# Output weights split beside two pairs of heads, and two output tiles split beside the last softmax sums, in a two-layer hybrid backbone

## The chip, the cores and the metric

One core of a Trainium2 chip runs the whole kernel in one launch. The metric is the device time of that launch in microseconds (us), the median of several runs. The engines are named as in the profile: PE is TensorE (PEld its weight loads, which overlap the matmuls), DVE is VectorE, ACT is ScalarE, POOL is GpSimd, and SP is the engine that only issues DMA transfers, in the order in which they stand in its queue.

## The reference, cut to what matters

The model has two layers. The change lies in the second half of the second one, attention over 1280 keys (256 of context, 1024 latent) for 1024 latent queries and 16 heads of 64 value columns:

```python
o = attend(q, k, v)                      # softmax(q k^T * SCALE) v, 16 heads
y = (o * silu(g)) @ w_out_mla            # 1024 x 1024
return layer_norm(ALPHA * h + gate * y, ln_g[1], ln_b[1])
```

Here `h` is the output of layer 0, itself a layer norm: `h = n * ln_g[0] + ln_b[0]`, with `n` kept in DRAM (`n_dr`).

## The kernel before, in words

All products that need float32 accuracy are made of three matmuls: an operand is split into a high part, rounded to the matmul's format (a cast, mostly on ACT), and a low part, the difference (a subtraction). The helper `split` (L80 to L82) does both, and `load` (L60) puts a DMA on SP's queue.

**Attention** runs over 8 pairs of heads (`p`), two halves of 512 queries (`hf`), and 10 key tiles (`kt`), so a pair has 20 steps (`g`). In a step `attend` (L1031) issues ten score matmuls into `s` (L1051), the exponential on ACT (`p`, L1053), and the running sum of the exponentials over the key tiles, which is the softmax's denominator: on POOL in pairs 0 to 6 (`ra`, L1057). In pair 7 the even key tiles are summed on POOL into `ra` and the odd ones on DVE into `rv` (L1061). Six buffers hold the exponentials. `pv` (L1064) multiplies them with the values into `po`. `finish` (L1070) gives the steps that end a half, done in the first steps of the next half: `rest` (the last two `pv`, and the gate `sgt` times `po` on DVE), `rows` (matmuls `rp` with ones that add the sums over the partitions, and a copy to `ri` on ACT), four `piece` (reciprocals on DVE), and `last` (`sgt` times `ri` on DVE, and the store to `o_dr` in DRAM).

Lists `near` and `far` hang other work on the steps. In pairs 0 to 6 this is the next pair's projections and its pass for the row maxima (`mx`, `m`). Pair 7 has no next pair; the **output weights** `wo1` are prepared there, in 8 slices of 128 rows: `wo1_load` (L1147) loads one, `wo1_high` (L1151) casts it on ACT, `wo1_low` (L1154) subtracts on POOL, or on DVE for three of the eight. They lie in the pool `fin1`, which takes the place of the projections' buffers.

**The output** has 8 tiles of 128 queries. `o_load` (L1103) reads a tile of all heads back from `o_dr` (`orw`), casts it (`oh`, ACT) and subtracts (`ol`, DVE). `out1` (L1185) is 48 matmuls into `yf` (L1191), 24 pairs of one for each half of the columns. Tile 0's load stands at the end of pair 7, and its matmuls are mixed with the steps that end the last half. All other buffers of this stage (the tiles' `oh` and `ol`, the residual `hres`, the vectors `g1bc`, `ln0`, `ln1`) are in the pool `fin`, which takes the place of attention's buffers. For each tile POOL makes the residual `hres` (L1216, L1217), and DVE makes `g1 * yf` (L1235), adds the residual (L1236), and norms (L1237 to L1246).

The order of PE, DVE, ACT and POOL in this part is the order in which the code issues (a manual schedule); SP's queue is ordered by the compiler's scheduler.

Of the kernel before, what the change touches and what calls it, by code (L numbers as in the profile page):

```python
# [54 lines left out]
def _body(ctx, tc, ap, out, dbg=None):  # L55
    nc = tc.nc
    V, S, G, TE = nc.vector, nc.scalar, nc.gpsimd, nc.tensor
    dbg = dbg or {}

    def load(o, i):  # L60
        nc.sync.dma_start(out=o, in_=i)

    def f(x):
        return x.bitcast(F32)

    def pool(name, bufs=1, space=None, side=None):
# [89 lines left out]
    gate_dr = dram.tile([2, 2, D], F32, name="gate_dr")  # L156
# [265 lines left out]
    for n in ("cos_h", "cos_l", "sin_h", "sin_l"):  # L422
        t = ft_p.tile([P, 2, 2, 256], F32R, name=n)
# [249 lines left out]
    qnh = [lat_p.tile([P, NL], F32R, name=f"qnh{k}") for k in range(2)]
    qnl = [lat_p.tile([P, NL], F32R, name=f"qnl{k}") for k in range(2)]
    kvh = lat_p.tile([P, T], F32R, name="kvh")
    kvl = lat_p.tile([P, T], F32R, name="kvl")
# [354 lines left out]
    def attend(p, hf, kt, st):  # L1031

        q, i = divmod(p, 2)
        c = slice(512 * hf, 512 * hf + 512)
        ks = slice(P * kt, P * kt + P)
        if kt == 0:
            st["sg"] = at.tile([P, 512], F32, tag="sgt", bufs=2, name=f"sgt{p}{hf}")
            load(st["sg"], sg_dr[p][:, c])
            st["o"] = o_ps.tile([P, 512], F32, tag="o", name=f"po{p}{hf}")
            st["ra"] = at.tile([P, 2, 512], F32, tag="ra", bufs=2, name=f"ra{p}{hf}")  # L1040
            if p == 7:
                st["rv"] = at.tile([P, 2, 512], F32, tag="rv", name=f"rv{hf}")
            st["e"] = []
        b = p % 2
        ps = s_ps.tile([P, 2, 512], F32, tag="s", name=f"s{p}{hf}{kt}")

        parts = ((Kh[b], Qh[b], 64), (Kh[b], Ql[b], 64), (Kl[b], Qh[b], 64), (KR1, R1[b], 64), (KR2, R2[b], 33))
        for j, (k, w, n) in enumerate(parts):
            for a in range(2):
                r = slice(64 * a, 64 * a + n)  # L1050
                TE.matmul(ps[:, a, :], k[r, ks], w[r, c], start=(j == 0), stop=(j == len(parts) - 1))  # L1051
        es = at.tile([P, 2, 512], F32, tag="p", bufs=PB, name=f"p{p}{hf}{kt}")
        S.activation(out=es, in_=ps, func=AF.Exp, scale=SCALE)  # L1053
        if kt:
            ra = st["ra"]
            if p < 7:
                G.tensor_tensor(out=ra, in0=st["e"][0] if kt == 1 else ra, in1=es, op=ALU.add)  # L1057
            elif kt > 1:

                ra = st["rv"] if kt % 2 else ra  # L1060
                (V if kt % 2 else G).tensor_tensor(out=ra, in0=st["e"][kt - 2] if kt < 4 else ra, in1=es, op=ALU.add)  # L1061
        st["e"].append(es)

    def pv(p, st, k):  # L1064
# [38 lines left out]
    def o_load(t, p):  # L1103
        orw = f1_p.tile([P, 8, P], F32, tag="raw", bufs=3, name=f"orw{t}")
        load(orw, o_dr.rearrange("k p t -> p k t")[:, :, P * t : P * t + P])
        oh = p.tile([P, 8, P], F32R, tag="oh", bufs=1 if t == 0 else 2, name=f"oh{t}")
        ol = p.tile([P, 8, P], F32R, tag="ol", bufs=1 if t == 0 else 2, name=f"ol{t}")
        split(oh, ol, orw, S, V)
        return oh, ol

    vt[1] = at.tile([P, NT, 256], F32, name="v_odd")
    tail = {}
    for p in range(8):

        near = [[] for _ in range(2 * NT)]
        far = [[] for _ in range(2 * NT)]
        if p < 7:
            prep = prep_pair(p + 1)
            mx = max_pass(p + 1)
            near[0] += prep[:2]  # L1120
            far[0] += prep[2:3]
            near[1] += prep[3:4]
            far[1] += prep[4:5]
            near[2] += prep[5:]
            at_ = [(g, b) for g in range(2, 2 * NT) for b in range(2) if not (g == 2 and b == 0) and (b == 0 or g % 2)]
            at_.insert(0, (2, 1))
# [12 lines left out]
        else:
            pr_c()  # L1140
            f1_p, f1_c = pool("fin1", 2, side="left")
            w1o = [f1_p.tile([P, D], F32R, bufs=1, name=f"w1oh{k}") for k in range(8)]
            w1p = [f1_p.tile([P, D], F32R, bufs=1, name=f"w1ol{k}") for k in range(8)]

            raws = {}

            def wo1_load(k):  # L1147
                raws[k] = f1_p.tile([P, D], F32, tag="raw", bufs=3, name=f"w1oraw{k}")
                load(raws[k], ap["wo1"][:, k, :])

            def wo1_high(k):  # L1151
                S.copy(out=w1o[k], in_=raws[k])

            def wo1_low(k):  # L1154
                (V if k % 3 == 1 else G).tensor_tensor(out=w1p[k], in0=raws[k], in1=f(w1o[k]), op=ALU.subtract)
                if k + 3 < 8:
                    wo1_load(k + 3)

            for k in range(3):
                wo1_load(k)  # L1160
            for k in range(8):
                far[2 * k + 2].append(lambda k=k: wo1_high(k))
                far[2 * k + 3].append(lambda k=k: wo1_low(k))
        for hf in range(2):
            st = {}
            for kt in range(NT):
                g = NT * hf + kt
                attend(p, hf, kt, st)
                for u in near[g]:
                    u()  # L1170
                if kt > 2 and kt % 2:
                    pv(p, st, kt - 3)
                    pv(p, st, kt - 2)
                for u in tail.get(kt, ()):
                    u()
                for u in far[g]:
                    u()
                if p == 7 and g == 18:
                    o0 = o_load(0, f1_p)
            tail = finish(p, hf, st)  # L1180

    s_psc()
# [2 lines left out]
    def out1(oh, ol, ps, pieces, group, work={}):  # L1185
        for k in range(8):
            for u in work.get(k, ()):
                u()
            for a, b in ((oh, w1o), (oh, w1p), (ol, w1o)):
                for i in group:  # L1190
                    TE.matmul(ps[i], a[:, k, :], b[k][:, pieces[i]],  # L1191
                              start=(k == 0 and a is oh and b is w1o), stop=(k == 7 and a is ol))

    H2 = [slice(0, 512), slice(512, D)]
    y0 = f_ps.tile([P, D], F32, tag="y", name="yf0")
    out1(*o0, [y0[:, c] for c in H2], H2, range(2), {1: tail[1], 3: tail[3]})
# [6 lines left out]

    fp, fc = pool("fin", 2, side="right")
    ln1 = fp.tile([P, 2, D], F32, bufs=1, name="ln1")
    ln0 = fp.tile([P, 2, D], F32, bufs=1, name="ln0")
    g1 = fp.tile([P, D], F32, bufs=1, name="g1bc")
    load(g1, gate_dr[1][0:1, :].to_broadcast([P, D]))
    for t in range(8):
        if t:  # L1210
            oh, ol = o_load(t, fp)
        x = fp.tile([P, D], F32, tag="hres", name=f"hres{t}")
        load(x, n_dr[t])
        if t == 0:
            load(ln0, ap["lnw0"].to_broadcast([P, 2, D]))
        G.tensor_tensor(out=x, in0=x, in1=ln0[:, 0, :], op=ALU.mult)  # L1216
        G.tensor_tensor(out=x, in0=x, in1=ln0[:, 1, :], op=ALU.add)  # L1217
        if t == 0:
            load(ln1, ap["lnw1"].to_broadcast([P, 2, D]))
# [23 lines left out]
        for hf in range(2):  # L1243
# [128 lines left out]
```

## Time and profile before

| | us |
|---|---|
| median of 3 runs | 1477.8 (1475.59 to 1479.57) |
| the profiled execution: its own time | 1479.07 |
| its span, first to last instruction | 1477.3 |
| PE busy (whole span) | 1409.1 (95%) |
| DVE busy | 931.4 (63%) |
| POOL busy | 660.9 (45%) |
| ACT busy | 539.9 (37%) |

The span ends with these stretches, counted from its start: pair 6 of attention from about 1240, pair 7 from about 1307 to 1352, the output tiles from 1357, the end at 1477.3. Shares over the whole span say little about the last 125 us, where other engines set the time than in the stretches before, so the rows below are taken from that part. A row of the timeline gives start, duration, engine, line, operation and names, and in brackets how long the engine was idle before it and what released it.

### The profile page before, as it was taken

What the parts mean: (1) busy time and instruction counts of PE and PEld (TensorE: products, weight loads), DVE (VectorE), ACT (ScalarE), POOL (GpSimd) and SP (SyncE); (2) the same over time, 40 slices, a digit from 0 to 9 for tenths busy, and PEclk for the clock granted to TensorE, in tenths of its full rate; (3) what the DMA queues carried; (4) which work ended last, traced back from release to release, by engine and by line L of the source; (5) the groups of instructions that cost most, each with busy time, mean ns of one, the idle gap of its engine ahead of it and who ended that gap; (6) DMA issues with size and microseconds to landing.
All of it is one profiled execution on the core that took longest, in us unless ns stands there. A gap on an engine that the chain in (4) does not pass through costs nothing.

```text
span 1477.3 us, 19801 instructions
## 1 busy us (share of the span) xinstructions
PE 1409.1 (95%) x7912; PEld 1009.3 (68%) x7912; DVE 931.4 (63%) x1461; ACT 539.9 (37%) x664; POOL 660.9 (45%) x307
## 2 busy tenths in 40 slices
PE   6998999999999999998999999999999999998895
PEld 3776777787888788887976755655555555554674
DVE  5668878665765352239635365667566665767698
ACT  2276566666112221105421333443433434353110
POOL 1134334343211143303241187568767856675442
PEclk9999999999999999999999999999999999999998
DMA  8613233332303564210242211012101101033431
GB/s 307 232 51 110 97 111 111 111 103 76 123 29 126 188 192 140 92 52 22 89 137 71 72 33 51 15 37 59 39 22 38 57 16 37 15 95 113 159 131 74
DMA packets 65868, 134.09 MB, mean 91 GB/s; under 512 B 5864, under 2 KB 31720, under 8 KB 63472
## 3 DMA queue, kind: packets, MB, share of 16 engines
q1 hardware_dynamic: 63328, 124.83, 26.1%
q0 software_dynamic: 2016, 7.60, 1.4%
q8 instruction: 62, 1.02, 0.3%
q10 hardware_dynamic: 432, 0.39, 0.1%
q14 instruction: 30, 0.25, 0.1%
HBM read 101.14 MB, written 24.66 MB: 85 GB/s over the span
## 4 chain that ended last, share of the span: by engine, by line
PE 68%; DVE 20%; DMA 4%; issue 4%; ACT 2%; POOL 2%; SPq 0%; DVEq 0%; POOLq 0%; ACTq 0%
PE s L1051 11%; PE z L267 11%; PE y L646 10%; PE po L1067 9%; PE mx L976 6%; PE in1g L85 2%; PE in1g L87 2%; PE in1g L86 2%; DVE xc L317 2%; DVE hf L1246 1%; DVE th L362 1%; DVE gate L367 1%; DVE gate L378 1%; DVE hf L1236 1%; DMA woraw<-in_wo 1%
## 5 line engine op out<-in xcount | busy, mean ns | idle before, releaser
L1057 POOL TENSOR_TENSOR ra<-ra,p 128x1024 f32<-128x1024 f32 x112 | 269.2, 2403 | 96.3 <-ACT p L1053 93.1
L978 DVE TENSOR_REDUCE m<-mx 128x1 f32<-128x512 f32 (+1 forms) x384 | 210.1, 589 | 100.9 <-PE mx L976 100.5
L1053 ACT ACTIVATE p<-s 128x1024 f32<-128x1024 f32 x160 | 163.3, 1025 | 208.4 <-PE s L1051 208.3
L267 PE MATMUL z<-uh,w0h 128*128 128x512 f32 (+1 forms) x576 | 150.1, 368 | 4.3 <-ACT uh L76 4.3
L267 PE MATMUL z<-ul,w0h 128*128 128x512 f32 (+1 forms) x576 | 147.9, 362 | 0.0
L267 PE MATMUL z<-uh,w0l 128*128 128x512 f32 (+1 forms) x576 | 147.5, 361 | 0.0
L82 POOL TENSOR_TENSOR w0l<-w,w0h 128x1024 fp32r<-128x1024 f32 x24 | 63.9, 2664 | 185.4 <-DVE w0h L78 135.5
L267 PEld LDWEIGHTS z<-uh,w0h 128*128 128x128 f32 x576 | 98.7, 191 | 33.4 <-issue 10.7
L267 PEld LDWEIGHTS z<-ul,w0h 128*128 128x128 f32 x576 | 96.8, 190 | 18.6 <-issue 1.0
L267 PEld LDWEIGHTS z<-uh,w0l 128*128 128x128 f32 x576 | 96.4, 190 | 18.3 <-issue 2.0
L1051 PE MATMUL s<-R,KR 33*128 33x512 f32 (+1 forms) x640 | 101.5, 392 | 0.0
L345 ACT ACTIVATE gate<-gps,vec 128x512 f32<-128x512 f32 (+1 forms) x96 | 57.5, 616 | 104.3 <-PE gps L87 104.2
L976 PE MATMUL mx<-Kh,Qh 64*128 64x512 f32 (+1 forms) x384 | 83.4, 404 | 4.5 <-DVE m L978 4.5
L976 PEld LDWEIGHTS mx<-Kh,Qh 64*128 64x128 f32 x384 | 39.1, 185 | 69.4 <-DVE m L978 35.5
L1067 PE MATMUL po<-p,v_odd 128*64 128x512 f32 x320 | 77.5, 605 | 0.0
L1067 PE MATMUL po<-p,v_even 128*64 128x512 f32 x320 | 77.5, 605 | 0.0
L381 POOL TENSOR_TENSOR gate<-gate,gate 128x1280 f32<-128x1280 f32 x8 | 23.9, 2988 | 112.2 <-DVE gate L378 97.1
L976 PE MATMUL mx<-KR,R 64*128 64x512 f32 (+1 forms) x384 | 72.7, 356 | 0.0
L1051 PEld LDWEIGHTS s<-R,KR 33*128 33x128 f32 (+1 forms) x640 | 61.3, 184 | 13.1
L1051 PE MATMUL s<-Qh,Kh 64*128 64x512 f32 x320 | 69.9, 430 | 0.0
L649 DVE TENSOR_TENSOR n<-gbc,y 128x1024 f32<-128x1024 f32 x10 | 12.2, 1222 | 86.1 <-PE y L646 86.1
L1051 PE MATMUL s<-Ql,Kh 64*128 64x512 f32 x320 | 63.7, 391 | 0.0
(360 smaller groups left out, 3078.0 us busy)
## 6 DMA issues: line engine op xcount, KB each, us to landing
w<-in_w SPq DMA_DIRECT2D x24, 512.0 KB
adaw<-in_ada SPq DMA_DIRECT2D x32, 256.0 KB
adawm<-in_ada SPq DMA_DIRECT2D x8, 1024.0 KB
adawg<-in_ada_g SPq DMA_DIRECT2D x8, 1024.0 KB
y_dr<-sg SPq DMA_DIRECT2D x10, 640.0 KB
woraw<-in_wo SPq DMA_DIRECT2D x12, 512.0 KB
xt<-in_x_cm SPq DMA_DIRECT2D x8, 640.0 KB
yra<-y_dr SPq DMA_DIRECT2D x10, 512.0 KB
```

Of the source, the lines that this page charges most:

```text
L82: el.tensor_tensor(out=lo, in0=src, in1=f(hi), op=ALU.subtract)
L85: TE.matmul(o, lh, rh, start=start, stop=False)
L86: TE.matmul(o, lh, rl, start=False, stop=False)
L267: TE.matmul(z[:, a : a + n], wi[:, kt, :], ui[kt][:, a : a + n], start=(kt == 0 and ui is uh and wi is wh), stop=(kt == KT - 1 and wi is wl))
L345: S.activation(out=gt[d, g][:, a : a + n], in_=ps[:, :n], func=AF.Sigmoid, bias=vv("gateb", 4 * j + i))
L646: TE.matmul(ps[:, 512 * hf : 512 * hf + 512], a[k], b[k][:, 512 * hf : 512 * hf + 512], start=(k == 0 and a is yh and b is woh), stop=(k = ...
L976: TE.matmul(ps[a][:, :n], q[r, P * t : P * t + P], k[r, a0 : a0 + n], start=st, stop=not st)
L978: V.tensor_reduce(out=m3s[t][:, a, i : i + 1], in_=ps[a][:, :n], axis=AX.X, op=ALU.max)
L1051: TE.matmul(ps[:, a, :], k[r, ks], w[r, c], start=(j == 0), stop=(j == len(parts) - 1))
L1053: S.activation(out=es, in_=ps, func=AF.Exp, scale=SCALE)
L1057: G.tensor_tensor(out=ra, in0=st["e"][0] if kt == 1 else ra, in1=es, op=ALU.add)
L1067: TE.matmul(st["o"][64 * a : 64 * a + 64, :], quad[q][6][:, k, 128 * i + 64 * a : 128 * i + 64 * a + 64], st["e"][k][:, a, :], start=(k == ...
```

## The change

The high and low parts of slices 0 to 2 of the output weights are put into the buffers of the normed latents (`qnh`, `qnl`, `kvh`, `kvl`), which pair 7's projections read last, at the start of pair 6. Slice 3 and the raw slices have a new pool `we`, beneath attention's buffers. So slices 0 to 3 are cast and subtracted in pair 6 (steps 5, 9, 13, 17 and the one after each), slices 4 to 7 in pair 7, and all eight subtractions are on POOL. In pair 7 the sums move: POOL adds key tiles 0, 1, 2, 4, 5, 6, 8 and DVE the tiles 3, 7, 9. The buffers of `oh`, `ol`, `hres`, `ln0` and `g1bc` move to `fin1`. Tile 1 is loaded and split inside tile 0's matmuls, and the residuals of tiles 0 and 1 are issued there. There are two raw buffers where there were three.

```diff
+    we_p, we_c = pool("we", side="right")
+    def wo1_high(k):
+        if k < 2:
+            hi, lo = (lat_p.tile([P, D], F32R, tag=f"qn{x}{k}", name=f"w1o{x}{k}") for x in "hl")
+        elif k == 2:
+            hi, lo = (lat_p.tile([P, T], F32R, tag=f"kv{x}", name=f"w1o{x}{k}")[:, :D] for x in "hl")
+        else:
+            hi, lo = ((we_p if k == 3 else f1_p).tile([P, D], F32R, bufs=1, name=f"w1o{x}{k}") for x in "hl")
+        w1o[k], w1p[k] = hi, lo
+        S.copy(out=hi, in_=raws[k])
+    def wo1_low(k):
+        G.tensor_tensor(out=w1p[k], in0=raws[k], in1=f(w1o[k]), op=ALU.subtract)
+        if k + 2 < 8:
+            wo1_load(k + 2)
...
-            if p < 7:
+            if p < 7 or kt == 1:
                 G.tensor_tensor(out=ra, in0=st["e"][0] if kt == 1 else ra, in1=es, op=ALU.add)
-            elif kt > 1:
-                ra = st["rv"] if kt % 2 else ra
-                (V if kt % 2 else G).tensor_tensor(out=ra, in0=st["e"][kt - 2] if kt < 4 else ra, in1=es, op=ALU.add)
+            elif kt > 1 and kt != 3:
+                e, r = (V, st["rv"]) if kt in (7, 9) else (G, ra)
+                e.tensor_tensor(out=r, in0=st["e"][3] if kt == 7 else r, in1=es, op=ALU.add)
...
+    def residual(t):
+        x = f1_p.tile([P, D], F32, tag="hres", name=f"hres{t}")
+        load(x, n_dr[t])
+        G.tensor_tensor(out=x, in0=x, in1=ln0[:, 0, :], op=ALU.mult)
+        G.tensor_tensor(out=x, in0=x, in1=ln0[:, 1, :], op=ALU.add)
+        return x
...
+            g1 = f1_p.tile([P, D], F32, bufs=1, name="g1bc")
+            load(g1, gate_dr[1][0:1, :].to_broadcast([P, D]))
+            ln0 = f1_p.tile([P, 2, D], F32, bufs=1, name="ln0")
+            load(ln0, ap["lnw0"].to_broadcast([P, 2, D]))
+        if p > 5:
+            for k in range(4 * (p - 6), 4 * (p - 6) + 4):
+                g = 5 + 4 * k if p == 6 else 3 * k - 10
+                far[g].append(lambda k=k: wo1_high(k))
+                far[g + 1].append(lambda k=k: wo1_low(k))
+            if p == 6:
+                near[3] += [lambda k=k: wo1_load(k) for k in range(2)]
...
-    out1(*o0, [y0[:, c] for c in H2], H2, range(2), {1: tail[1], 3: tail[3]})
+    def second():
+        os_[1] = o_load(1)
+    out1(*os_[0], [y0[:, c] for c in H2], H2, range(2), {1: tail[1] + [second], 3: tail[3]})
+    xs = {t: residual(t) for t in range(2)}
```

PE's rows are the same, in the same order. Three places show what moves on the others. The first is DVE in pair 7, from the end of pair 6 to the first output tile's low part; names ending in 11209 (before) and 11222 (changed) are the gate of pair 7's first half. Before:

```order
L1061 TENSOR_TENSOR rv_11213<-rv_11213,p_11390 128x1024
L1077 TENSOR_TENSOR sgt_11209<-sgt_11209,po_11211 128x512
L1155 TENSOR_TENSOR w1ol_11199<-w1oraw_11322,w1oh_11191 128x1024
L1061 TENSOR_TENSOR rv_11404<-p_11430,p_11473 128x1024
L1092 RECIPROCAL ri_11459<-ri_11459 128x128 x3
L1061 TENSOR_TENSOR rv_11404<-rv_11404,p_11510 128x1024
L1092 RECIPROCAL ri_11459<-ri_11459 128x128
L1096 TENSOR_TENSOR sgt_11209<-ri_11459,sgt_11209 128x512
```

In the changed kernel, from the same `rv` on:

```order
L1083 TENSOR_TENSOR rv_11226<-rv_11226,p_11405 128x1024
L1099 TENSOR_TENSOR sgt_11222<-sgt_11222,po_11224 128x512
L1114 RECIPROCAL ri_11472<-ri_11472 128x128 x4
L1118 TENSOR_TENSOR sgt_11222<-ri_11472,sgt_11222 128x512
L1083 TENSOR_TENSOR rv_11417<-p_11486,p_11555 128x1024
L82 TENSOR_TENSOR ol_11579<-orw_11576,oh_11578 128x1024
```

A weight's subtraction and two sums that stood between the gate's two products are gone from there. The second place is POOL in pair 7, up to the first sum of its second half. Before (five of the rows; the first half's sum is `ra_11212`):

```order
L1061 TENSOR_TENSOR ra_11212<-p_11225,p_11256 128x1024
L1155 TENSOR_TENSOR w1ol_11195<-w1oraw_11203,w1oh_11187 128x1024
L1061 TENSOR_TENSOR ra_11212<-ra_11212,p_11297 128x1024
L1061 TENSOR_TENSOR ra_11212<-ra_11212,p_11335 128x1024
L1155 TENSOR_TENSOR w1ol_11197<-w1oraw_11207,w1oh_11189 128x1024
L1061 TENSOR_TENSOR ra_11212<-ra_11212,p_11373 128x1024
L1155 TENSOR_TENSOR w1ol_11198<-w1oraw_11284,w1oh_11190 128x1024
```

Changed, with the last subtraction of pair 6 ahead of it:

```order
L1043 TENSOR_TENSOR w1ol_11169<-w1oraw_10941,w1oh_11168 128x1024
L1079 TENSOR_TENSOR ra_10917<-ra_10917,p_11207 128x1024
L1079 TENSOR_TENSOR ra_11225<-p_11238,p_11251 128x1024
L1083 TENSOR_TENSOR ra_11225<-ra_11225,p_11270 128x1024
L1043 TENSOR_TENSOR w1ol_11274<-w1oraw_11070,w1oh_11273 128x1024
L1083 TENSOR_TENSOR ra_11225<-ra_11225,p_11312 128x1024
L1083 TENSOR_TENSOR ra_11225<-ra_11225,p_11327 128x1024
L1083 TENSOR_TENSOR ra_11225<-ra_11225,p_11349 128x1024
L1043 TENSOR_TENSOR w1ol_11336<-w1oraw_11194,w1oh_11335 128x1024
L1083 TENSOR_TENSOR ra_11225<-ra_11225,p_11386 128x1024
```

The half's sum now needs six adds with two subtractions among them, where it needed four and two. The third place is SP's queue where attention begins, around the store of the last gate (`sg_71`). Before:

```order
L61 DMA sg_dr<-sg_70_6591 128x512
L61 DMA sgt_6682<-sg_dr 128x512
L61 DMA R_6666<-roth_5789 32x1024 x2
L61 DMA sg_dr<-sg_71_6652 128x512
L61 DMA R_6667<-rotl_5790 32x1024
```

Changed:

```order
L61 DMA sg_dr<-sg_70_6591 128x512
L61 DMA w1oraw_10703<-in_wo 128x1024
L61 DMA w1oraw_10705<-in_wo 128x1024
L61 DMA sg_dr<-sg_71_6652 128x512
L61 DMA sgt_6685<-sg_dr 128x512
L61 DMA R_6669<-roth_5789 32x1024 x2
L61 DMA R_6670<-rotl_5790 32x1024
```

The first two weight slices are loaded there, and the rotary queries of pair 1 (`R`) now stand behind the store.

## Rows read from the trace of the kernel before

**Rows 1.** Windows: start:end, us, busy us (count) PE, PEld, DVE, ACT, POOL, clock, DMA share, GB/s

```profile
1240.00:1307.00 67.00, 66.42 (x438) 38.06 (x434) 41.01 (x74) 25.98 (x29) 47.51 (x20) 1.00 0.13 38
1307.00:1352.00 45.00, 44.95 (x276) 21.93 (x272) 36.36 (x22) 26.53 (x29) 35.41 (x14) 1.00 0.34 110
1352.00:1357.20 5.20, 0.00 (x0) 0.00 (x0) 2.37 (x1) 1.06 (x2) 1.29 (x1) 0.96 0.80 218
1357.20:1362.00 4.80, 4.76 (x14) 2.35 (x14) 2.36 (x2) 0.91 (x1) 0.00 (x0) 0.68 0.74 198
1432.00:1444.00 12.00, 11.85 (x51) 9.28 (x50) 11.96 (x14) 1.24 (x2) 5.51 (x3) 1.00 0.25 88
```

**Rows 2.** The chain that ended last, 1348 to 1392: start us, us, what

```profile
1348.06 1.91 DVE sgt L1096
...
1349.98 2.00 DMA o_dr<-sgt
...
1352.06 4.06 DMA orw<-o_dr
...
1356.14 1.05 ACT oh L76
...
1357.24 2.93 PE yf L1191 x6
...
1367.56 3.40 DVE ri L1092 x4
...
1374.03 7.62 DMA ln<-in_lnw
...
1386.72 5.68 DVE hf L1236 x2
```

**Rows 3.** Timeline of PE, from pair 7's first denominator to the fourth output tile's start

```profile
1333.33 1.08 PE L1084 MATMUL rp<-ra,ones 128*64 128x512 f32 x4
...
1350.01 1.94 PE L1067 MATMUL po<-p,v_odd 128*64 128x512 f32 x8
1357.24 1.22 PE L1191 MATMUL yf<-w1oh,oh 128*128 128x512 f32 x2 [5.29 <-ACT oh L76]
...
1373.81 0.63 PE L1191 MATMUL yf<-w1oh,oh 128*128 128x512 f32 x2
...
1396.21 0.63 PE L1191 MATMUL yf<-w1oh,oh 128*128 128x512 f32 x2
```

**Rows 4.** Timeline of DVE: a sum of pair 7, and steps of output tiles

```profile
1343.80 3.36 DVE L1061 TENSOR_TENSOR rv<-rv,p 128x1024 f32<-128x1024 f32 x1
...
1423.41 1.27 DVE L1235 TENSOR_TENSOR hf<-g1bc,yf 128x512 f32<-128x512 f32 x2
...
1453.70 5.71 DVE L1246 SCALAR_TENSOR_TENSOR hf<-hf,rsb,ln 128x512 f32<-128x512 f32 x2
...
1459.33 1.27 DVE L1235 TENSOR_TENSOR hf<-g1bc,yf 128x512 f32<-128x512 f32 x2
...
1464.67 1.41 DVE L1246 SCALAR_TENSOR_TENSOR hf<-hf,rsb,ln 128x512 f32<-128x512 f32 x2
```

**Rows 5.** Timeline of POOL, from pair 6's last sums to pair 7's last

```profile
1302.53 4.83 POOL L1057 TENSOR_TENSOR ra<-ra,p 128x1024 f32<-128x1024 f32 x2 [0.71 <-ACT p L1053]
...
1346.03 3.38 POOL L1061 TENSOR_TENSOR ra<-ra,p 128x1024 f32<-128x1024 f32 x1
1350.45 2.85 POOL L1061 TENSOR_TENSOR ra<-ra,p 128x1024 f32<-128x1024 f32 x1 [1.04 <-ACT p L1053]
```

**Rows 6.** Timeline of ACT in pair 7

```profile
1335.53 0.59 ACT L1087 COPY ri<-rp 128x512 f32<-128x512 f32 x1 [1.00 <-PE rp L1084]
...
1349.28 1.03 ACT L1053 ACTIVATE p<-s 128x1024 f32<-128x1024 f32 x1 [1.81 <-PE s L1051]
```

**Rows 7.** Timeline of SP's queue where attention begins

```profile
845.79 0.59 SPq L61 DMA_DIRECT2D R<-rotl  x1
```

**Rows 8.** Timeline of PE there: the first product with R

```profile
851.32 0.40 PE L976 MATMUL mx<-KR,R 64*128 64x512 f32 x2
```

More of the change, by code (lines that the diff above doesn't have):

```diff
@@ L672, in _body @@
     lat_p, lat_c = pool("lat", side="right")
[L673 to L676, printed above, removed]
+    qnh = [lat_p.tile([P, NL], F32R, tag=f"qnh{k}", name=f"qnh{k}") for k in range(2)]
+    qnl = [lat_p.tile([P, NL], F32R, tag=f"qnl{k}", name=f"qnl{k}") for k in range(2)]
+    kvh = lat_p.tile([P, T], F32R, tag="kvh", name="kvh")
+    kvl = lat_p.tile([P, T], F32R, tag="kvl", name="kvl")
     u1_p, u1_c = pool("u1", side="right")
@@ L1023, in _body, with wo1_load @@
     u1_c()
+    we_p, we_c = pool("we", side="right")
+    w1o, w1p, raws = {}, {}, {}
+    def wo1_load(k):
+        raws[k] = we_p.tile([P, D], F32, tag="raw", bufs=2, name=f"w1oraw{k}")
+        load(raws[k], ap["wo1"][:, k, :])
+    def wo1_high(k):
[11 more added lines that the diff above has]
+            wo1_load(k + 2)
     at, at_c = pool("at", side="right")
@@ L1101, in finish, with o_load @@
         return {1: [rest], 3: [rows], 4: [piece(0)], 5: [piece(1)], 6: [piece(2)], 7: [piece(3)], 8: [last]}
-    def o_load(t, p):
-        orw = f1_p.tile([P, 8, P], F32, tag="raw", bufs=3, name=f"orw{t}")
+    def o_load(t):
+        orw = we_p.tile([P, 8, P], F32, tag="raw", bufs=2, name=f"orw{t}")
         load(orw, o_dr.rearrange("k p t -> p k t")[:, :, P * t : P * t + P])
-        oh = p.tile([P, 8, P], F32R, tag="oh", bufs=1 if t == 0 else 2, name=f"oh{t}")
-        ol = p.tile([P, 8, P], F32R, tag="ol", bufs=1 if t == 0 else 2, name=f"ol{t}")
+        oh = f1_p.tile([P, 8, P], F32R, tag="oh", name=f"oh{t}")
+        ol = f1_p.tile([P, 8, P], F32R, tag="ol", name=f"ol{t}")
         split(oh, ol, orw, S, V)
         return oh, ol
+    def residual(t):
[4 more added lines that the diff above has]
+        return x
     vt[1] = at.tile([P, NT, 256], F32, name="v_odd")
@@ L1141, in _body @@
             f1_p, f1_c = pool("fin1", 2, side="left")
[L1142 to L1163, printed above, removed]
+            g1 = f1_p.tile([P, D], F32, bufs=1, name="g1bc")
[9 more added lines that the diff above has]
+                near[3] += [lambda k=k: wo1_load(k) for k in range(2)]
         for hf in range(2):
@@ L1178, in _body @@
                 if p == 7 and g == 18:
-                    o0 = o_load(0, f1_p)
+                    os_ = {0: o_load(0)}
             tail = finish(p, hf, st)
@@ L1205, in _body @@
     ln1 = fp.tile([P, 2, D], F32, bufs=1, name="ln1")
-    ln0 = fp.tile([P, 2, D], F32, bufs=1, name="ln0")
-    g1 = fp.tile([P, D], F32, bufs=1, name="g1bc")
-    load(g1, gate_dr[1][0:1, :].to_broadcast([P, D]))
+    load(ln1, ap["lnw1"].to_broadcast([P, 2, D]))
     for t in range(8):
[L1210 to L1219, printed above, removed]
+        oh, ol = os_.pop(t) if t in os_ else o_load(t)
+        x = xs.pop(t) if t in xs else residual(t)
         h = fp.tile([P, D], F32, tag="h", name=f"hf{t}")
@@ L1248, in _body @@
     fc()
+    we_c()
     f1_c()
```

## The prediction

> **What bounds the kernel now.** I read the windows first, for who is busy in each stretch. In pairs 6 and 7 TensorE works without a gap (66.42 of 67 us, 44.95 of 45), so nothing that shortens another engine's work there shortens the pair. From 1352.0 to 1357.2 TensorE does nothing; in the 4.8 us behind that gap its granted clock is 0.68, a mix of the levels 1.2 and 2.4 GHz, against 1.00 before. In an output tile of the steady end VectorE is busy 11.96 of 12 us and TensorE 11.85 [rows 1].
>
> The chain of waits says what the gap is made of. The gate of pair 7's first half leaves VectorE at 1349.97, its store takes 2.00 us, the load of tile 0 4.06, the cast 1.05; the first six matmuls of tile 0 then need 2.93 us. Further on the chain waits 7.62 us for the norm vectors `ln`, and VectorE's first step that needs the residual starts at 1386.72 [rows 2], though TensorE had tile 0 ready at 1373.81, where tile 1 begins [rows 3]. So the end has two late points: tile 0 itself, and its residual, 12.9 us later.
>
> The timeline gives the rates. TensorE starts tile 1 at 1373.81 and tile 3 at 1396.21, so a tile is 11.20 us, and a pair of matmuls 11.20/24 = 0.467 [rows 3]. VectorE starts the chain of a tile at 1423.41 and that of the third after it at 1459.33: 11.97 us a tile, more than TensorE's 11.20. From the start of the seventh chain, at 1459.33, to the end of the span 1477.3 there are 17.97 us [rows 4]. VectorE sets the end, counted from the time at which it can begin tile 0.
>
> **The gap ahead of tile 0 (removed).** Pair 7's first denominator is multiplied from 1333.33 on [rows 3] and copied by 1336.12 [rows 6]. Before, VectorE has a weight's subtraction and two sums among the four reciprocals. Now the four follow each other: 3.40 us [rows 2], to 1339.5. The gate's product took 1.91 us beside GpSimd [rows 2]; with a further wait for GpSimd's operation I allow it until 1342.4. Store and load (2.00 + 4.06) put the tile at 1348.5. ScalarE reaches the cast after the exponential that ends at 1350.31 [rows 6], and is done at 1351.4. TensorE's last `po` ends at 1351.95 [rows 3]. The load has 1.8 us to spare and the cast 0.6, so the gap of 5.29 us goes [rows 3], and with it the slow clock: 2.93 − 6 × 0.233 = 1.53 us [rows 2, 3]. Together 6.82.
>
> **A new wait: tile 0's low part.** It moves to the time of GpSimd's last sum, which starts at 1350.45 [rows 5]. The two engines take turns: a sum on VectorE that starts at 1343.80 takes 3.36 us, to 1347.16, and the GpSimd sum that starts at 1346.03 takes 3.38, because VectorE's own 1.1 us falls into it [rows 4, 5]; 3.38 less that 1.1 leaves 2.3, near the 2.41 of each of two undisturbed sums (4.83 for two) [rows 5]. So `ol` runs when GpSimd is done, 1352.85, and ends at 1353.95. TensorE wants it after two pairs, at 1351.95 + 0.93 = 1352.9: 1.1 us lost, and behind it wait only `po` and the rest of the tile. Bounds: 0 if VectorE goes first, 2.4 if GpSimd takes another operation first (the first residual is queued there). I take 1.1. The Trainium skill, page "SBUF — State Buffer", section "SBUF: two separate sides", says that GpSimd and a VectorE operation with two SBUF inputs share one port pair by a lock held for the whole instruction, and that whoever starts first blocks the other. The rows agree; by that rule alone, with GpSimd at the lock from the exponential's end on, the wait is the same 1.1, and each further GpSimd operation that I move beside VectorE would cost it up to 2.4.
>
> Tile 0 thus ends on TensorE 6.82 − 1.1 = 5.7 us earlier, at 1368.1.
>
> **The residual of tile 0 (moved).** `g1bc`, `ln0` and the two `hres` loads are issued in pair 7 and no longer wait for attention's buffers; issued from about 1310 on, even at 7.62 us each, one after the other, they are there by 1341. GpSimd's four operations follow its last sum: 1352.9 + 4 × 2.41 + turns for `ol`, `rv` and tile 1's `ol` (3.3) = 1365.8, before 1368.1. Only `ln1` still waits for attention's buffers; it is issued behind the last gate's store, about 1366 (the reciprocals' 1367.56 less 5.7, their 3.40 and the product [rows 2]), and at 7.62 us lands at 1374, where VectorE needs it some 5 us after its start (three times two operations of 1.27 [rows 4] and a low part of 1.1), 1373.3: 0 to 1 us, taken as 0. So VectorE begins tile 0 at about 1368.4.
>
> **The sum.** 1368.4 + 6 × 11.97 + 17.97 = 1458.2 for the span, 19.1 less than 1477.3. TensorE stays ahead: tile 1 ends at 1379.3, VectorE takes it at 1380.4, and 0.8 us more are gained by each further tile. Two raw buffers instead of three make the load of tile t + 2 wait for the low part of tile t; the low parts of these two are 24 us apart, a load and a cast 5.1. The own time of the profiled execution, 1479.07, becomes 1460.0; the median is 1.27 lower, so I forecast 1477.8 − 19.1, rounded to **1459**.
>
> **Edits costed at nothing.** In pair 6 four casts (1.05 each [rows 2]) go to ScalarE, busy 25.98 of 67 us, and four subtractions of 2.4, 9.7 in all, to GpSimd, busy 47.51 [rows 1]; the cover is their idle time. The last subtraction pushes pair 6's end on GpSimd from 1307.4 [rows 5] to 1309.8. Uncovered, they would cost 2.4 for the one that stands ahead of a denominator. In pair 7 GpSimd has 16 operations of 2.4, 38.5 of 45 us. By turns with VectorE (two sums, one product) the first half's sum is done at about 1331, 2.4 before TensorE wants it at 1333.33. On SP's queue in pair 6 the third to fifth slices stand ahead of pair 7's row maxima; the fifth waits for GpSimd at step 14 of 20, the maxima come after step 18, some 13 us later at 3.35 us a step [rows 1]. The sixth waits for the end of the last subtraction in pair 6, with the first gate of pair 7 behind it, needed 22 us later. At the start of attention the last load of `R` was issued by 846.4 [rows 7]; behind the last gate's store it is about 1.5 us later, 847.9. Landing takes between 2.0, as the store, and 7.62, as the vectors [rows 2], so 849.9 to 855.5 against 851.32, when TensorE wants it [rows 8]. 128 KB beside little else is nearer the store: nothing, at most 4.2.
>
> **The rivals.** *A late feeder.* The same end, but TensorE waits in attention: for `R` (up to 4.2, and 1.5 of slow clock), or for the first half's sum in pair 7. If GpSimd's last five operations ahead of it took 3.38 [rows 5] instead of 2.4, it would come 4.9 later and 2.5 too late, and the load of tile 0 just after the last `po`. Either costs about 5: **1464**. For it: the margins, 1.4 and 2.4, are small. Against: VectorE keeps half of its two-input operations there.
>
> *TensorE sets the pace of the tiles.* A norm's second product takes 5.71 us for two beside GpSimd and 1.41 alone [rows 4]. If the residuals shift to where VectorE reads PSUM, its tile falls below 11.20, and the end is 6 × 0.77 = 4.6 earlier: **1454**. Against: the residual's load still starts when VectorE has read the last but one, as in every tile before.
>
> *VectorE starts late again*, since a load (`ln1`, or a residual behind it) holds tile 0. With the 5.7 us of tile 0 alone the end is at 1471.6, and the median at **1472**.
>
> *Slower.* With two raw buffers each tile's load could stand on VectorE's path: a tile would take 11.97 + 4.06 + 1.05 = 17.1, seven of them 36 more than forecast: **1495**. It decides when a load lands over 20 us after the low part that frees its buffer; 7.62 is the longest seen [rows 2].
>
> **The numbers.** My forecast 0.66 (own range 1456 to 1462: `ol` 0 to 2.4, `ln1` 1, the rounding of starts), late feeder 0.13, TensorE's pace 0.11, late start 0.07, slower 0.03. 1453 to 1466 leaves out the last two and some late feeders, under 0.2. A change of 0.3% (4.4 us) is what a measurement here can tell from none: faster 0.94, same 0.03 (half a late start with a late feeder), slower 0.03.
>
> **What would show it.** Right: no idle stretch of TensorE over 2 us between the last `po` and tile 3; clock 1.00 there; VectorE's first `hf` at 1368 to 1370, its step with the residual right behind, and 12 us from tile to tile. Wrong: an idle TensorE at 851 or 1333; pairs 6 and 7 longer than 112 us; VectorE waiting for `ln` or `hres`; a tile other than 12 us.

## The result, and the profile after

| | us |
|---|---|
| before, median of 4 runs | 1478.68 (1475.59 to 1482.18) |
| after, median of 4 runs | 1454.44 (1450.71 to 1457.82) |
| after, the profiled execution: own time, span | 1450.71, 1448.9 |

The ratio is 0.9833, 95% interval 0.9806 to 0.9860: 24 us faster, where 19 were forecast. The windows of the changed kernel, with the columns of [rows 1]: pair 6, pair 7, the first matmuls of tile 0, and an output tile of the steady end.

```profile
1234.00:1301.00 67.00, 67.00 (x444) 38.66 (x444) 42.55 (x76) 30.59 (x34) 53.87 (x24) 1.00 0.19 56
1301.00:1346.00 45.00, 45.00 (x276) 22.39 (x275) 17.21 (x16) 25.60 (x28) 44.45 (x18) 1.00 0.43 141
1346.00:1351.00 5.00, 3.87 (x16) 1.60 (x15) 5.00 (x2) 0.60 (x1) 4.92 (x3) 1.00 0.37 102
1400.00:1412.00 12.00, 12.00 (x54) 9.74 (x53) 11.96 (x15) 1.34 (x2) 5.50 (x2) 1.00 0.40 132
```

In pair 7 DVE's busy time has halved (36.36 to 17.21 us) and POOL is full (35.41 to 44.45 of 45). The idle 5.2 us and the slow clock of [rows 1] are gone: the clock is 1.00 in all four windows.

The timeline of PE, from pair 7's first denominator to the start of tile 1, which answers to [rows 3]:

```profile
1327.30 1.08 PE L1106 MATMUL rp<-ra,ones 128*64 128x512 f32 x4
...
1343.79 1.94 PE L1089 MATMUL po<-p,v_odd 128*64 128x512 f32 x8
1345.65 0.73 PE L1210 MATMUL yf<-w1oh,oh 128*128 128x512 f32 x2
...
1347.99 0.72 PE L1210 MATMUL yf<-w1oh,ol 128*128 128x512 f32 x2 [1.13 <-DVE ol L82]
...
1362.35 0.63 PE L1210 MATMUL yf<-w1oh,oh 128*128 128x512 f32 x2
```

Tile 0 starts straight behind the last `po`. The idle 5.29 us are gone; in their place stands a new wait of 1.13, for the low part `ol`. The timeline of DVE in that stretch and in the tiles, which answers to [rows 4], and then that of POOL ([rows 5]):

```profile
1329.91 3.39 DVE L1114 RECIPROCAL ri<-ri 128x128 f32<-128x128 f32 x4 [3.17 <-ACT ri L1109]
1333.33 0.69 DVE L1118 TENSOR_TENSOR sgt<-ri,sgt 128x512 f32<-128x512 f32 x1
...
1344.83 3.11 DVE L82 TENSOR_TENSOR ol<-orw,oh 128x1024 fp32r<-128x1024 f32 x1 [2.69 <-ACT oh L76]
...
1362.61 1.28 DVE L1249 TENSOR_TENSOR hf<-g1bc,yf 128x512 f32<-128x512 f32 x2 [2.38 <-PE yf L1210]
1363.81 1.29 DVE L1250 SCALAR_TENSOR_TENSOR hf<-hres,hf 128x512 f32<-128x512 f32 x2
...
1373.64 1.28 DVE L1249 TENSOR_TENSOR hf<-g1bc,yf 128x512 f32<-128x512 f32 x2 [0.99 <-PE yf L1210]
...
1403.94 5.69 DVE L1260 SCALAR_TENSOR_TENSOR hf<-hf,rsb,ln 128x512 f32<-128x512 f32 x2
1409.56 1.27 DVE L1249 TENSOR_TENSOR hf<-g1bc,yf 128x512 f32<-128x512 f32 x2
...
1415.90 3.57 DVE L1260 SCALAR_TENSOR_TENSOR hf<-hf,rsb,ln 128x512 f32<-128x512 f32 x2
1419.39 1.27 DVE L1249 TENSOR_TENSOR hf<-g1bc,yf 128x512 f32<-128x512 f32 x2
...
1430.22 1.27 DVE L1249 TENSOR_TENSOR hf<-g1bc,yf 128x512 f32<-128x512 f32 x2
```

POOL in the same stretch:

```profile
1336.22 10.63 POOL L1083 TENSOR_TENSOR ra<-ra,p 128x1024 f32<-128x1024 f32 x4
1346.80 3.35 POOL L1136 TENSOR_TENSOR hres<-hres,ln 128x1024 f32<-128x1024 f32 x1
...
1356.90 2.40 POOL L1137 TENSOR_TENSOR hres<-hres,ln 128x1024 f32<-128x1024 f32 x1
...
1403.51 2.77 POOL L1136 TENSOR_TENSOR hres<-hres,ln 128x1024 f32<-128x1024 f32 x1 [6.39 <-DVE rsb L1256]
...
1415.93 2.98 POOL L1136 TENSOR_TENSOR hres<-hres,ln 128x1024 f32<-128x1024 f32 x1 [6.85 <-DMA hres<-n_dr]
```

The reader is to see four things: the reciprocals and the gate's product follow each other with nothing between; `ol` takes 3.11 us, 2.0 of them until POOL's last sum ends at 1346.85; DVE's step with the residual (L1250) follows the first step of tile 0 (L1249) at once; and a tile is usually 12 us, but 11.03 for the first, 9.83 and 10.83 for the fifth and sixth.

**Where the 28.4 us between the two profiled executions lie.** The span is cut in three: up to the first score matmul `s` of attention, from there to the end of the last `po` ahead of tile 0 ("attention"), and the rest ("the end stage"). Before these are 841.66, 510.29 and 125.35 us, after 840.12, 505.61 and 103.17. So 1.54 us are from ahead of attention, 4.68 from attention, 22.18 from the end stage. Of attention's, 1.13 are three small steps in pairs 5 to 7, most of it one wait for `m` in pair 6 (at 1276.55 before), which the kernel with the weights alone, below, has lost too. The other 3.55 are two steps, of 1.8 us each, in pairs 0 and 2, where the change does nothing. The first, before:

```profile
862.53 2.72 DVE L882 TENSOR_SCALAR wk<-wk,vec 128x512 f32<-128x512 f32 x1
862.58 2.39 POOL L1057 TENSOR_TENSOR ra<-ra,p 128x1024 f32<-128x1024 f32 x1
...
865.91 0.49 PE L976 MATMUL mx<-Kh,Qh 64*128 64x512 f32 x1 [1.27 <-DVE m L978]
```

and after:

```profile
861.03 0.48 DVE L882 TENSOR_SCALAR wk<-wk,vec 128x512 f32<-128x512 f32 x1
...
861.08 2.68 POOL L1079 TENSOR_TENSOR ra<-ra,p 128x1024 f32<-128x1024 f32 x1
```

DVE scales the key weights `wk` in pairs 0, 2 and 4, each time some 0.05 us ahead of a sum on POOL. It takes 0.48 us or, held by that sum, 2.72; then the row maxima `m` are late and PE waits. Before, all three were long; after, only the third. Whether that belongs to the change is the first question below.

### The profile page after: what moved, and what is told of

Its sections match the earlier page's. It is cut to its first block, busy times and chain, and to the rows that moved or that the text cites. A ratio compares the mean times of both kernels' runs of the same rounds, so it can differ in the third digit from the quotient of the medians.

```text
span 1448.9 us, 19809 instructions
## 1 busy us (share of the span) xinstructions
PE 1402.8 (97%) x7912; PEld 1005.8 (69%) x7912; DVE 903.4 (62%) x1454; ACT 541.3 (37%) x664; POOL 678.5 (47%) x314
## 4 chain that ended last, share of the span: by engine, by line
PE 73%; DVE 17%; issue 3%; DMA 3%; ACT 2%; POOL 1%; SPq 0%; DVEq 0%; POOLq 0%; ACTq 0%
PE s L1073 13%; PE z L267 11%; PE y L646 10%; PE po L1089 10%; PE mx L976 6%; PE in1g L85 2%; PE in1g L87 2%; PE in1g L86 2%; DVE xc L317 2%; PE yf L1210 2%; DVE gate L367 1%; DVE th L362 1%; DVE hf L1260 1%; DVE gate L378 1%; PE rp L1106 1%
## 5 line engine op out<-in xcount | busy, mean ns | idle before, releaser
L1114 DVE RECIPROCAL ri<-ri 128x128 f32<-128x128 f32 x64 | 59.4, 938 | 9.9 <-ACT ri L1109 9.9
```

Source lines behind the costliest of these rows:

```text
L1114: V.reciprocal(out=st["ri"][:, d], in_=st["ri"][:, d])
```

## The experiments

All profiles in one table, as above. "Long" counts the scalings of `wk` that took 2.7 us. Each ratio is to runs of the kernel before on the same chip, whose medians were 1478.7 to 1482.4, so ratios compare better than medians.

| kernel | start | long | attention | end stage | span | median us | ratio to before (95%) |
|---|---|---|---|---|---|---|---|
| before | 841.66 | 3 | 510.29 | 125.35 | 1477.3 | 1478.7 | |
| changed | 840.12 | 1 | 505.61 | 103.17 | 1448.9 | 1454.4 | 0.9833 (0.9806 to 0.9860) |
| changed, again | 839.85 | 2 | 507.28 | 104.37 | 1451.5 | 1455.3 | 0.9816 (0.9795 to 0.9837) |
| `wk` on ACT | 841.31 | none | 503.89 | 104.30 | 1449.5 | 1453.0 | 0.9801 (0.9780 to 0.9822) |
| before, `wk` on ACT | 839.93 | none | 504.86 | 126.71 | 1471.5 | 1474.2 | 0.9958 (0.9943 to 0.9973) |
| weights only | 840.37 | 3 | 509.17 | 123.56 | 1473.1 | 1474.6 | 0.9945 (0.9924 to 0.9966) |
| weights, sums | 843.98 | 3 | 511.15 | 119.47 | 1474.6 | 1474.0 | 0.9950 (0.9930 to 0.9970) |
| weights, residual | 842.41 | 3 | 511.04 | 106.45 | 1459.9 | 1461.6 | 0.9867 (0.9852 to 0.9882) |
| no early tile 1 | 842.65 | 3 | 511.17 | 104.58 | 1458.4 | 1460.5 | 0.9860 (0.9839 to 0.9881) |
| `ol` last | 843.12 | 2 | 507.41 | 103.77 | 1454.3 | 1458.5 | 0.9836 (0.9815 to 0.9857) |
| chain in PSUM | 841.89 | 3 | 509.13 | 102.88 | 1453.9 | 1454.4 | 0.9814 (0.9790 to 0.9837) |
| three edits | 839.93 | none | 504.02 | 101.15 | 1445.1 | 1447.2 | 0.9775 (0.9759 to 0.9791) |

**The changed kernel once more.**

> The changed kernel once more, unchanged. Theory (the steps upstream are VectorE's scaling of the key weights `wk`, which takes 0.48 us or, when GpSimd's sum starts at the same moment, 2.72, and then holds TensorE 1.8 us): each of the three scalings in attention is either 0.48 or 2.72, each long one costs some 1.8 us, and the time stays within 1450 to 1458 with the rest of the trace the same: 103 us from the end of the last `po` to the end of the span. Rival (the spread lies in the output tiles): the stretch after the last `po` differs by several us between the two executions and attention does not.

Two scalings are long (993.41 and 1127.82, 2.73 each), attention is 1.67 us longer than in the first profile. The end stage differs by 1.2: one of its tiles is short (9.82 us) where the first profile had two. So both theories hold a part: some 1.7 of a difference of 2.6 lie in attention.

**The scaling of `wk` on ACT**, in the changed kernel and in the kernel before.

```diff
-            V.tensor_scalar(out=u, in0=u, scalar1=vv("kvng"), scalar2=None, op0=ALU.mult)
+            S.activation(out=u, in_=u, func=AF.Copy, scale=vv("kvng"))
```

> The scaling of `wk` moved from VectorE to ScalarE. Theory (VectorE's scaling is blocked by GpSimd's sum): no step of 1.8 us is left in attention, each product `mx` behind it starts without a wait, and the time is 2 to 5 us under the changed kernel's, about 1451, with a smaller spread. Rival (the steps come from when the loads are issued, or move to the cast that follows on ScalarE): the time stays within 1 us of the changed kernel's, and TensorE still waits for `m` or for a late exponential at the same places.

> The kernel before, with only the scaling of `wk` moved to ScalarE. Theory (VectorE's scaling, blocked by GpSimd's sum, costs TensorE 1.8 us each time and has nothing to do with the change): the three waits of `mx` for `m` in attention are gone, attention takes 510.3 - 3 x 1.8 = 505 us instead of 510.3, everything behind the last `po` stays (125 us), and the time falls by 3 to 6 us. Rival (the change's own loads at attention's start are what removed these waits in the changed kernel's first profile): the waits stay, and the time is within 2 us of the kernel before.

Before: attention falls from 510.29 to 504.86 (505 was expected), the end stage does not gain (126.71), and the time falls by 5.3 us. After: attention is 503.89, 1.7 less than with one long scaling and 3.4 less than with two; the medians differ by 2.3 with overlapping intervals, so the gain there is read from the trace, not from the times. The rival falls in both: the scaling itself makes the step, and it is in the kernel before as well as in the changed one. Between the two kernels without it the medians differ by 21.2 us (the ratios by 1.57%, 23 us) and the end stages by 22.4: that is the change's own worth.

**The change in parts.** All three kernels keep the split beside pair 6. The first and third put pair 7's sums, and two low halves, back on DVE; the first and second make the residual (and load its vectors) where the kernel before does, and leave tile 1 unsplit. The core of the two edits:

```diff
-            if p < 7 or kt == 1:
+            if p < 7:
...
-                e, r = (V, st["rv"]) if kt in (7, 9) else (G, ra)
+                ra = st["rv"] if kt % 2 else ra
...
-        G.tensor_tensor(out=w1p[k], in0=raws[k], in1=f(w1o[k]), op=ALU.subtract)
+        (V if k in (4, 7) else G).tensor_tensor(out=w1p[k], in0=raws[k], in1=f(w1o[k]), op=ALU.subtract)
```

```diff
-    xs = {t: residual(t) for t in range(2)}
+    xs = {}
...
-    load(ln1, ap["lnw1"].to_broadcast([P, 2, D]))
+    ln0 = fp.tile([P, 2, D], F32, bufs=1, name="ln0")
+    g1 = fp.tile([P, D], F32, bufs=1, name="g1bc")
+    load(g1, gate_dr[1][0:1, :].to_broadcast([P, D]))
```

> Of the change only the split of half of the weights beside pair 6 is kept; pair 7's sums and two of its low halves go back to VectorE, and the residual, its vectors and tile 1 are prepared where the kernel before does it. Theory (the gain comes from the gate of pair 7 and from the early residual): the gap ahead of tile 0 is back, about 5 us, VectorE gets its residual some 12 us after TensorE has finished tile 0, and the stretch from the end of the last `po` to the end of the span is 125 us, as before; the time is 1 to 3 us under the kernel before, from pair 6. Rival (moving the splits is itself the gain, since ScalarE and VectorE are freer in pair 7): no gap, and 115 to 120 us.

> The split beside pair 6 and the new places of pair 7's sums are kept; the residual, its vectors and tile 1 are prepared as in the kernel before. Theory (two late points in a row, each with its own price): the gap is gone and tile 0 ends 5.7 us earlier, VectorE still waits some 12 us for the residual, and the stretch behind the last `po` is 125.35 - 5.7 = 119.6 us, or 117 to 120 with a short tile. Rival (the residual, not the gap, sets the end, so that closing the gap alone gives nothing): 124 to 125. Rival 2 (TensorE's pace sets the end and VectorE catches up): 110 or less.

> The split beside pair 6 and the early residual are kept; pair 7's sums and two low halves go back to VectorE as in the kernel before. Theory: the gap ahead of tile 0 is back with the slow clock behind it, the wait for `ol` is gone, VectorE has its residual when tile 0 ends, and the stretch behind the last `po` is 103 to 104 + 5.3 + 1.4 - 1.1 = 109 to 110 us. Rival (the reciprocals are late for another reason than VectorE's sums and low halves): no gap, 103 to 104.

PE's timeline of the kernel with the weights only, at tile 0, and its chain of waits behind it:

```profile
1351.38 0.74 PE L1209 MATMUL yf<-w1oh,oh 128*128 128x512 f32 x2 [1.84 <-ACT oh L76]
```

```profile
1367.75 9.69 DMA ln<-in_lnw
...
1382.50 5.68 DVE hf L1248 x2
```

The gap is there, but 1.84 us and not 5: the rival is right for two thirds of the gap, though not for the end stage (123.56, where it said 115 to 120). With four subtractions fewer in pair 7 the gate's product ends 5.6 us ahead of the last `po`'s end, where it ended 2.0 ahead in [rows 2, 3]. DVE still has a subtraction and two sums between the gate's two products, but POOL has no subtraction beside them any more:

```profile
1339.95 2.44 DVE L1083 TENSOR_TENSOR rv<-rv,p 128x1024 f32<-128x1024 f32 x1 [0.65 <-ACT p L1075]
...
1343.28 0.69 DVE L1118 TENSOR_TENSOR sgt<-ri,sgt 128x512 f32<-128x512 f32 x1
```

This sum and the product took 3.36 and 1.91 us before [rows 2, 4]. The time falls by 6.6 us on that chip (1481.3 to 1474.6), where 1 to 3 were expected; in the profiles the end stage and attention hold 2.9 of it, and the rest is not explained. The residual is as late as before. With the sums moved too, the gap is gone and the end stage is 119.47, where the theory said 119.6; the residual's wait is still there. The chain of that kernel:

```profile
1354.17 3.19 DVE ol L82
1357.40 0.72 PE yf L1209 x2
...
1371.02 8.24 DMA ln<-in_lnw
...
1384.31 5.68 DVE hf L1248 x2
```

With the early residual but the old sums the gap is 1.95 and `ol` costs 0.89; the end stage is 106.45 instead of the 109 to 110 expected, since the gap has only that size. So in the end stage the sums give 4.1 us with a late residual and 2.1 to 3.3 with an early one, the residual 17.1 with the old sums and 15.1 to 16.3 with the new, and the weights alone 1.8, with 1.1 more in attention. The medians show these parts less clearly: the sums alone give nothing there (1474.6 and 1474.0; in the profiles attention is 2.0 us longer and the start 3.6 beside the shorter end stage), and the residual with the old sums gives 13.0 (1474.6 to 1461.6). So the sizes are those of the end stage in one profile each. The residual's part is larger than its delay, which was 12.9 in the kernel before. The rows suggest why, though no run tests it alone: when it is late, tile 0's step with it (5.68 for two) also stands by turns with POOL's work on tile 1's residual, where the changed kernel takes 1.29, 4.4 us less.

**No early tile 1.**

```diff
-    def second():
-        os_[1] = o_load(1)
-
-    out1(*os_[0], [y0[:, c] for c in H2], H2, range(2), {1: tail[1] + [second], 3: tail[3]})
+    out1(*os_[0], [y0[:, c] for c in H2], H2, range(2), {1: tail[1], 3: tail[3]})
```

> The changed kernel without the early split of tile 1: its load, cast and low part stand in the loop, behind the two residuals. Theory (TensorE works on tile 0 for 16.6 us, time enough to load and split tile 1 later; the value of the change is in tile 0 and the residual): TensorE starts tile 1 without a wait, and the stretch behind the last `po` stays at 103 to 104.4 us. Rival (the load then stands behind the last gate's store and tile 0's chain holds the split): TensorE waits 2 to 5 us ahead of tile 1 and the stretch is 105 to 109.

PE does not wait ahead of tile 1, and the end stage is 104.58, 0.2 from the second profile of the changed kernel: this part of the change is worth nothing that shows there. The median is 1460.5 all the same, 5 to 6 us over the changed kernel's two. Its profile has three long scalings and, behind the third, a slow clock, which the two kernels with 511 us of attention above share. The windows of the kernel with weights and sums, behind its wait of 1.31 us for `m` at 1137.10:

```profile
1136.00:1139.00 3.00, 1.90 (x7) 0.74 (x9) 3.00 (x6) 2.45 (x3) 1.99 (x3) 0.84 0.00 0
1139.00:1142.00 3.00, 3.00 (x14) 1.06 (x12) 1.69 (x4) 0.00 (x0) 2.92 (x2) 0.59 0.00 0
1142.00:1145.00 3.00, 3.00 (x21) 1.97 (x18) 2.29 (x6) 1.02 (x1) 2.01 (x2) 1.00 0.00 0
```

A granted clock of 0.59 is a mix that is mostly the level of 1.2 GHz. It makes that step 2.0 us longer. Six other profiles have a long scaling at the same place without it; what decides that stays open, and so does whether the edit has a part in it.

**Tile 0's low products last.**

```diff
...
-            for a, b in ((oh, w1o), (oh, w1p), (ol, w1o)):
...
+        three = (oh, w1o), (oh, w1p), (ol, w1o)
+        order = [(k, a, b) for k in range(8) for a, b in (three[:2] if work else three)]
+        order += [(k, ol, w1o) for k in range(8) if work]
...
```

> In tile 0 alone the eight products with the low part of the activations stand behind all others. Theory (tile 0's low part `ol` costs 1.1 us on the path): TensorE has no idle time behind the first pairs of `yf`, tile 1 starts 16.6 - 1.1 = 15.5 us after the last `po`, VectorE's chain starts 1.1 earlier, and the time is about 1.1 us under the changed kernel's, 1453.3. Rival (the residual or the norm vectors hold VectorE there): VectorE's first `hf` starts earlier but its next step waits by as much, and the time is the same.

No product waits for `ol`, and PE is through with all tiles 93.3 us after the last `po`, where it was 94.7 in the changed kernel. But the end stage is 103.77, between those of the changed kernel's two profiles, and the median, 1458.5, is not under theirs: the span now ends 10.4 us behind PE's last product instead of 8.5 and 9.7. The expected 1.1 us are given back by DVE, the rival's answer, though at another place than the rival put it. DVE in tile 0:

```profile
1366.07 1.23 DVE L82 TENSOR_TENSOR ol<-orw,oh 128x1024 fp32r<-128x1024 f32 x1 [1.45 <-PE yf L1213]
1367.22 1.28 DVE L1251 TENSOR_TENSOR hf<-g1bc,yf 128x512 f32<-128x512 f32 x2
```

The first row is the low part of tile 2. It takes the buffer of tile 0's low part, which PE now reads up to the last product of tile 0, and it stands ahead of tile 0's first `hf`. So that step starts 16.69 us after the last `po`, where it started after 16.88. Against the changed kernel's second profile (104.37), which has the same short tile near its end, 0.6 us of the end stage are gained.

**The output chain in PSUM.**

```diff
...
-                V.scalar_tensor_tensor(out=h[:, c], in0=x[:, c], scalar=ALPHA, in1=h[:, c], op0=ALU.mult, op1=ALU.add)
+                V.scalar_tensor_tensor(out=ps[i], in0=x[:, c], scalar=ALPHA, in1=ps[i], op0=ALU.mult, op1=ALU.add)
...
-            V.scalar_tensor_tensor(out=h[:, c], in0=h[:, c], scalar=rs, in1=ln1[:, 1, c], op0=ALU.mult, op1=ALU.add)
+            V.scalar_tensor_tensor(out=h[:, c], in0=ps[i], scalar=rs, in1=ln1[:, 1, c], op0=ALU.mult, op1=ALU.add)
```

> The chain of an output tile works in the PSUM buffer in place of `hf`, so that no VectorE step of it has two SBUF inputs. Theory (the tile's 11.97 us on VectorE are made by turns with GpSimd's residual; the two tiles of 9.8 and 10.8 had none): no step of the chain takes more than 1.5 us for two, VectorE waits for TensorE at each tile, tiles follow each other at TensorE's 11.2, and the end comes some 5.5 us behind TensorE's last product at 1440.8, so about 2.6 us earlier than in the changed kernel: 1452. Rival (PSUM operands are slower, or the buffer held longer stops TensorE): tiles of 12 us or more, or a TensorE that waits ahead of tiles 2 to 7, and 1455 to 1465.

DVE in one of its tiles; POOL works on a residual from 1398.21 to 1403.09 and from 1410.35 on:

```profile
1401.13 0.70 DVE L1249 TENSOR_TENSOR yf<-g1bc,yf 128x512 f32<-128x512 f32 x1 [2.20 <-PE yf L1210]
1401.80 2.38 DVE L82 TENSOR_TENSOR ol<-orw,oh 128x1024 fp32r<-128x1024 f32 x1
...
1408.84 0.75 DVE L1259 SCALAR_TENSOR_TENSOR hf<-yf,rsb,ln 128x512 f32<-128x512 f32 x1
...
1410.42 0.75 DVE L1259 SCALAR_TENSOR_TENSOR hf<-yf,rsb,ln 128x512 f32<-128x512 f32 x1
```

The theory holds in the tile: with one input in PSUM no step is held by POOL (0.75 beside it at 1410.42, and no step of the chain over 0.76, where two steps with both inputs in SBUF take 5.69), DVE waits for PE, and the tiles come at PE's pace. Only `ol`, with both inputs in SBUF, is still held. The Trainium skill, page "SBUF — State Buffer", section "Who interferes with whom", says that a DVE instruction with at most one SBUF input does not contend with GpSimd outside its two-port modes, and that the scaling with one input (`tensor_scalar`) can be in such a mode; both agree with these rows and those of `wk`. The gain is 0.3 to 1.5 us in the end stage, not 2.6, since the span, which ended 8.5 and 9.7 us behind PE's last product, still ends 7.8 behind it, where 5.5 were expected, and PE's last product comes 0.4 later; the medians show no gain.

**Three edits together:** `wk` on ACT, `ol` last, the chain in PSUM.

> The changed kernel with the scaling of `wk` on ScalarE, tile 0's low products last, and the output tiles' chain in PSUM. Theory (TensorE now sets the end, so only together do an earlier tile 0 and a shorter VectorE chain pay): attention takes 504 us from its first product to the last `po`, no product of `yf` waits for `ol`, and the stretch behind it is 102.9 - 1.2 = 101.7; with a start at 840 to 843 the time is 1447 to 1450, median 1449, 5 to 6 us under the changed kernel's. Rival (VectorE's `ol`, still by turns with GpSimd, takes the place of what was removed): the stretch stays at 103 to 104 and the time at 1451 to 1453.

Attention is 504.02 (504 expected), the end stage 101.15 (101.7), the time 1447.2 us: 7 to 8 us under the changed kernel's two medians (6 to 9 by the ratios), with an interval that touches neither of theirs, and so faster than both kernels. The chain of waits of its end:

```profile
1343.95 1.60 PE yf L1213 x6
1345.55 1.87 PE po L1089 x8
1347.42 3.00 PE yf L1213 x12
1350.41 1.87 PE rp L1106 x8
1352.28 84.99 PE yf L1213 x390
...
1441.65 0.48 DVE hf L1261
```

From the last `po` to its last product PE waits for nothing. `ol` last alone gave 0.6 at most in the end stage and the chain in PSUM 0.3 to 1.5; together they give 2.0 to 3.2 (103.17 and 104.37 to 101.15): one makes PE earlier, the other lets DVE follow.

## Why the prediction was right, and where its sizes were off

The median, 1454.4, is 4.6 us under the forecast, below its own range of 1456 to 1462 and at the number of the rival *TensorE's pace* (1454). The mechanism is the forecast's all the same, and that the number is the rival's is in part luck: of the 9.3 us by which the profiled execution is under its own forecast, half lies in stages that the change does not touch (last paragraph of this part). Of the signs of being wrong one came, a tile other than 12 us.

**The bound and the two late points: right.** The end is counted from DVE's start on tile 0. The parts bear out both points: 119.47 us with the residual alone late is 0.2 from the rival *VectorE starts late again* (1471.6 less 1351.95).

**The gap (6.82 us): right, its margin was larger.** The gate's product ends 11.7 us ahead of the last `po`'s end, where the forecast had 9.6: it took 0.69, as it started 0.06 us ahead of POOL's subtraction, and there was no further wait for POOL. In the kernels with `ol` last and with the chain in PSUM it was held, took 2.94 us and ended 9.5 ahead, as forecast. The experiments split the gap differently from the text: the text named the subtraction and the sums that stand on DVE; with the weights moved first, their leaving pair 7 gives 3.45 of 5.29, mostly as POOL's turns, and the sums 1.84. The sums without the weights were not run.

**The new wait for `ol` (1.1 us): right**, 1.11 to 1.14 in the six profiles that have the new sums and not `ol` last. By turns, as said: `ol` ends 1.1 us behind the end of POOL's last sum, 1346.85. What it is worth at the end was not: with the wait gone DVE comes to tile 0 only 0.2 us earlier.

**The residual: right.** POOL's four operations end at 1359.30, 13.6 us after the last `po`'s end (forecast 13.85), and DVE does not wait for `hres` or `ln`. DVE starts tile 0 16.88 us after the last `po`, where the forecast had 16.45.

**The pace of the tiles: the term that was mis-sized.** Six spacings of 11.97 are 71.8; measured are 67.61 and 68.75. The first spacing is 11.03 in one profile and 11.04 in the other: in tile 0 the last product is held once (3.55), not twice. And near the end one or two tiles are short. At 1415.90 DVE's last product starts 0.03 us ahead of POOL's residual and is held once (3.57 for 5.69), where it usually starts 0.4 us behind it (1403.94 and 1403.51). Most of that is the residual's load, which was issued 0.33 us later; SP's queue shows it:

```profile
1400.15 0.33 SPq L61 DMA_DIRECT2D hres<-n_dr  x1
...
1412.45 0.33 SPq L61 DMA_DIRECT2D hres<-n_dr  x1
```

The two issues are 12.30 us apart and not 11.97; why is left open. That is the rival *TensorE's pace* in part: it was said that the residuals could shift, and they do, by tenths of a microsecond. With the tail (18.68 for 17.97) the end stage is 103.17, 3.1 less than the forecast 106.25.

**The edits at nothing: right in pairs 6 and 7 and at attention's start.** PE waits neither for the first half's sum at 1327.30 nor for `R`; *late feeder* did not come, nor *slower*: no tile waits for its load. A gain of 1.1 us in pairs 5 to 7 was not seen ahead: PE's 66.42 of 67 us in pair 6 were called work without a gap, but the 0.58 us are a wait for `m`, and it is gone (67.00 of 67).

**Not in the prediction at all: the scaling of `wk`.** The forecast in the terms of its own profile was 1460.0 against 1450.71, and the 9.3 us between are 3.1 from the end stage, 1.1 from pairs 5 to 7, 3.55 from two scalings and 1.5 from ahead of attention. Which scalings are held differs between executions of one kernel, so that part is luck. What varies ahead of attention (839.85 to 843.98 in the table) is in large part one wait of PE at about 513 us, for the cast `woh` in layer 0: 0.66 us in the changed kernel's second profile, 2.75 in the kernel with weights and sums, where a granted clock of 0.60 follows. Why it varies is left open.

## What to carry to other kernels

When a kernel has two late points in a row, price each from the point where the next engine could begin, and add what its lateness makes collide: here 12.9 us of delay were 15 to 17 us of the end stage. Before a difference is put down to a change, cut both traces at the same landmarks and look at stages that the change doesn't touch: here 5 of 28 us came from there. Once two engines are this close to each other, an edit to one can show next to nothing: here the two had to be made together.

## What the runs showed of the hardware that was not expected

Of two instructions that start 0.05 us apart on DVE and POOL either can be held: of the three scalings of `wk` in attention, in nine profiles with them on DVE, 23 of 27 were held for POOL's whole operation (2.7 us) and 4 were not (0.48). DVE's row starts first in all of them, by 50 to 61 ns in the four and by 31 to 47 ns in the 23, so the order of the starts in a trace does not tell who was held, while the lead, in these 27, does: some hundredths of a microsecond decide. It is not one lead for all: the gate's product in pair 7 went first with 16 to 62 ns in eight profiles of kernels with the moved weights, and was held with 2 and -17 in the other two. One scaling that is held costs 1.8 us, so executions of one program differ by it with no other cause in sight (attention took 505.61 and 507.28 us in the two profiles of the changed kernel); and of the 23 waits of PE, 1.3 us each in stretches where it is otherwise full, three were followed by the slow clock, each in a profile of its own and after the third scaling, and cost 2.0 us more.
